# A ring of three-group blocks under the framework's own dependencies in place of hand-made semaphores

## The chip, the cores and the metric

The kernel runs on one core of a Trainium2 chip. The metric is the device time of one execution, in microseconds (us); lower is better. A run that lies over 1.5% above the fastest run of its kernel in the same job counts as slow, and the comparisons use the other, fast, runs.

## The reference, cut to what matters

```python
B, S, D = 8, 4096, 2112          # x is float32
x_r = x.reshape(B, S // 4, 4, D)
pooled = x_r.mean(axis=2)
return x - np.repeat(pooled, 4, axis=1)
```

Four neighbouring rows are averaged and the average is taken off each of them. Input and output are 276.8 MB each.

## The kernel before

A *group* is 128 x 4 rows: each of the 128 partitions holds four rows of 2112 numbers side by side (`W` = 8448). There are 64 groups. SBUF holds a ring of six of them. Three adjacent groups form a *block*, which is loaded and stored in two *pieces* of one and a half groups (6.49 MB each); so the ring holds four pieces. The last four groups go one by one.

```python
blocks = [SUPER] * ((n - TAIL) // SUPER)      # SUPER = 3, TAIL = 4: twenty blocks of three
blocks += [1] * (n - sum(blocks))             # and four singles
...
ring = io_pool.tile([P, RING * W], f32, name="ring")       # RING = 6
s_sb = sum_pool.tile([P, D], f32, name="s_sb")             # sums of even groups, in SBUF
s_ps = psum_pool.tile([P, D], f32, name="s_ps")            # sums of odd groups, in PSUM
```

Loads are issued by SP, stores by ACT, and VectorE (DVE) does all the arithmetic: per group three adds and one *sub*, which multiplies the sum by -1/4 and adds it to the four rows in place. Every wait is written by hand, inside a section that the framework does not touch:

```python
for i, (a, b, src, _, _) in enumerate(moves):          # one load per piece
    ...
    load = nc.sync.dma_start(out=ring[:, a:b], in_=src)
    load._wait_ge(*landed(store_sems, m))              # m: the store that empties this piece
    load.then_inc(load_sems[i % SEMS], 16)
...
for j, (c, need) in enumerate(groups):
    s = s_ps if j % 2 else s_sb
    add = nc.vector.tensor_add(out=s[:], in0=rows[:, 0, :], in1=rows[:, 1, :])
    if need > seen:
        add._wait_ge(*landed(load_sems, need))
    ...                                                # two more adds
    sub = nc.vector.scalar_tensor_tensor(out=rows, in0=..., scalar=-1.0 / STRIDE, in1=rows, ...)
    ...
    store._wait_ge(done_sem, done)                     # a piece leaves when its last sub is done
```

In this section instructions run in the order in which they are written.

## Time and profile before

| | before |
|---|---|
| median of the three runs first made | 1318.18 us (1297.61 to 1322.84) |
| profiled run, span | 1288.6 us |
| VectorE busy | 1023.0 us, 79% |
| load queue + store queue | 49.8% + 49.6% of the DMA engines' time |
| rate, 336 to 1056 us | 434 GB/s |

The lines behind this table are shown in the prediction.

### The profile page before, as it was taken

The numbers are of one execution on the slowest core, as the hardware profiler recorded it, in microseconds if no ns is written. First come the engines' busy times: TensorE is split into PE (matmuls) and PEld (weight loads), VectorE is DVE, ScalarE is ACT, GpSimd is POOL, SyncE is SP. The second block draws the span as 40 slices with busy tenths as digits, with TensorE's granted clock in tenths as the row PEclk, the third lists the DMA queues.
The fourth block names the chain that finished last, engine by engine and source line by source line (L and its number), as shares of the span: only waits on it lengthen the run. The fifth ranks groups of instructions, "written<-read, shape, count | busy, mean of one in ns | idle before, by whom it ended". The sixth has DMA issues, their size and how long they took to land.

```text
span 1288.6 us, 398 instructions
## 1 busy us (share of the span) xinstructions
DVE 1023.0 (79%) x256; POOL 0.2 (0%) x4
## 2 busy tenths in 40 slices
DVE  4999696786969696969688696969696968779864
POOL 0000000000000000000000000000000000000000
DMA  9999999999999999999999999999999999999997
GB/s 403 428 428 434 439 436 428 428 439 437 431 430 434 441 433 428 433 439 434 431 431 439 436 431 430 437 438 431 430 434 442 431 430 431 437 437 425 429 428 325
DMA packets 12674, 553.67 MB, mean 430 GB/s; under 512 B 1408, under 2 KB 1408, under 8 KB 1408
## 3 DMA queue, kind: packets, MB, share of 16 engines
q1 hardware_dynamic: 6336, 276.83, 49.8%
q10 hardware_dynamic: 6336, 276.83, 49.6%
q14 instruction: 2, 0.02, 0.0%
HBM read 276.82 MB, written 276.82 MB: 430 GB/s over the span
## 4 chain that ended last, share of the span: by engine, by line
DMA 66%; DVE 27%; another core or an unknown queue 6%; issue 0%; SPq 0%
DMA out_dram<-ring 35%; DMA ring<-in_x_dram 30%; DVE ring L115 15%; DVE s_ps L111 4%; DVE s_sb L111 4%; DVE s_ps L103 2%; DVE s_sb L103 2%; SPq L89 0%; SPq L161 0%; SPq L80 0%
## 5 line engine op out<-in xcount | busy, mean ns | idle before, releaser
L115 DVE SCALAR_TENSOR_TENSOR ring<-s_sb,ring 128x8448 f32<-128x8448 f32 x32 | 286.7, 8958 | 1.1
L115 DVE SCALAR_TENSOR_TENSOR ring<-s_ps,ring 128x8448 f32<-128x8448 f32 x32 | 286.6, 8957 | 1.1
L103 DVE TENSOR_TENSOR s_sb<-ring 128x2112 f32<-128x2112 f32 x32 | 75.2, 2351 | 132.0 <-DMA ring<-in_x_dram 132.0
L103 DVE TENSOR_TENSOR s_ps<-ring 128x2112 f32<-128x2112 f32 x32 | 75.6, 2362 | 114.3 <-DMA ring<-in_x_dram 114.3
L111 DVE TENSOR_TENSOR s_ps<-s_ps,ring 128x2112 f32<-128x2112 f32 x64 | 151.4, 2366 | 2.2
L111 DVE TENSOR_TENSOR s_sb<-s_sb,ring 128x2112 f32<-128x2112 f32 x64 | 150.9, 2358 | 2.2
L150 POOL MEMSET const-bfloat16-1.0<- 128x1 bf16 x1 | 0.1, 103 | 0.0
L150 POOL MEMSET const-uint8-127<- 128x1 uint8 x1 | 0.1, 102 | 0.0
L150 POOL MEMSET const-float32-0.0<- 128x1 f32 x1 | 0.1, 100 | 0.2 <-issue 0.2
L150 POOL MEMSET const-float32-1.0<- 128x1 f32 x1 | 0.1, 99 | 0.0
## 6 DMA issues: line engine op xcount, KB each, us to landing
ring<-in_x_dram SPq DMA_DIRECT2D x40, 6336.0 KB, 37.4
out_dram<-ring ACTq DMA_DIRECT2D x40, 6336.0 KB, 37.7
ring<-in_x_dram SPq DMA_DIRECT2D x4, 4224.0 KB, 42.7
out_dram<-ring ACTq DMA_DIRECT2D x4, 4224.0 KB, 29.2
```

What stands on the lines that cost most here:

```text
L103: add = nc.vector.tensor_add(out=s[:], in0=rows[:, 0, :], in1=rows[:, 1, :])
L111: add = nc.vector.tensor_add(out=s[:], in0=s[:], in1=rows[:, f, :])
L115: sub = nc.vector.scalar_tensor_tensor(out=rows, in0=s[:, None, :].to_broadcast([P, STRIDE, D]), scalar=-1.0 / STRIDE, in1=rows, op0=mybir ...
L150: nc = _bacc.Bacc("TRN2", target_bir_lowering=False, num_devices=1)
```

## The change

The intent is to hand all synchronization to the framework, which derives waits from what each instruction reads and writes, and to make 21 blocks of three with one single at the end. The diff, cut to its core:

```diff
-TAIL = 4
-SEMS = 8
+TAIL = 1
...
-    with tc.tile_critical():
-        ...                                  # owners, waits and semaphores by hand
+    done = stored = 0
+    for i, (a, b, src, _, _) in enumerate(moves):
+        nc.sync.dma_start(out=ring[:, a:b], in_=src)
+        while done < len(groups) and groups[done][1] <= i:
+            ...
+            s = s_ps if done % 2 else s_sb
+            nc.vector.tensor_add(out=s[:], in0=rows[:, 0, :], in1=rows[:, 1, :])
             for f in range(2, STRIDE):
-                add = nc.vector.tensor_add(out=s[:], in0=s[:], in1=rows[:, f, :])
-                add._wait_ge(done_sem, done)
-                add.then_inc(done_sem)
+                nc.vector.tensor_add(out=s[:], in0=s[:], in1=rows[:, f, :])
-            sub = nc.vector.scalar_tensor_tensor(
+            nc.vector.scalar_tensor_tensor(
                 ...
             )
+            done += 1
+            while stored < len(moves) and moves[stored][4] < done:
+                a, b, _, dst, _ = moves[stored]
+                nc.scalar.dma_start(out=dst, in_=ring[:, a:b])
+                stored += 1
```

Outside the hand-made section the framework also chooses the order of instructions on an engine.

More of the change, by code (lines that the diff above doesn't have):

```diff
@@ L71 @@
     s_ps = psum_pool.tile([P, D], f32, name="s_ps")
-    load_sems = [tc.alloc_semaphore(f"load{i}") for i in range(SEMS)]
-    store_sems = [tc.alloc_semaphore(f"store{i}") for i in range(SEMS)]
-    done_sem = tc.alloc_semaphore("done")
-    def landed(sems, i):
-        return sems[i % SEMS], 16 * (i // SEMS + 1)
-    with tc.tile_critical():
-        owner = {}
-        free = set()
-        for i, (a, b, src, _, _) in enumerate(moves):
-            taken = sorted(
-                {m for (p, q), m in owner.items() if p < b and a < q} - free
-            )
-            for m in taken[:-1]:
-                nc.sync.wait_ge(*landed(store_sems, m))
-            load = nc.sync.dma_start(out=ring[:, a:b], in_=src)
-            for m in taken[-1:]:
-                load._wait_ge(*landed(store_sems, m))
-            load.then_inc(load_sems[i % SEMS], 16)
-            free.update(taken)
-            owner = {c: m for c, m in owner.items() if m not in free}
-            owner[(a, b)] = i
-        done = 0
-        seen = -1
-        stored = 0
-        for j, (c, need) in enumerate(groups):
-            rows = ring[:, c:c + W].rearrange("p (f d) -> p f d", f=STRIDE)
-            s = s_ps if j % 2 else s_sb
-            add = nc.vector.tensor_add(out=s[:], in0=rows[:, 0, :], in1=rows[:, 1, :])
-            assert need <= seen + 1
-            if need > seen:
-                add._wait_ge(*landed(load_sems, need))
-                seen = need
-            add.then_inc(done_sem)
-            done += 1
-            for f in range(2, STRIDE):
-                add = nc.vector.tensor_add(out=s[:], in0=s[:], in1=rows[:, f, :])
-                add._wait_ge(done_sem, done)
-                add.then_inc(done_sem)
-                done += 1
-            sub = nc.vector.scalar_tensor_tensor(
@@ new lines @@
+    done = stored = 0
+    for i, (a, b, src, _, _) in enumerate(moves):
+        nc.sync.dma_start(out=ring[:, a:b], in_=src)
+        while done < len(groups) and groups[done][1] <= i:
+            c = groups[done][0]
+            rows = ring[:, c:c + W].rearrange("p (f d) -> p f d", f=STRIDE)
+            s = s_ps if done % 2 else s_sb
+            nc.vector.tensor_add(out=s[:], in0=rows[:, 0, :], in1=rows[:, 1, :])
+            for f in range(2, STRIDE):
+                nc.vector.tensor_add(out=s[:], in0=s[:], in1=rows[:, f, :])
+            nc.vector.scalar_tensor_tensor(
@@ L122 @@
             )
-            sub._wait_ge(done_sem, done)
-            sub.then_inc(done_sem)
             done += 1
-            while stored < len(moves) and moves[stored][4] <= j:
+            while stored < len(moves) and moves[stored][4] < done:
                 a, b, _, dst, _ = moves[stored]
-                store = nc.scalar.dma_start(out=dst, in_=ring[:, a:b])
-                store._wait_ge(done_sem, done)
-                store.then_inc(store_sems[stored % SEMS], 16)
+                nc.scalar.dma_start(out=dst, in_=ring[:, a:b])
                 stored += 1
-        assert stored == len(moves)
-        for m in sorted(set(range(len(moves))) - free):
-            nc.sync.wait_ge(*landed(store_sems, m))
+    assert done == len(groups) and stored == len(moves)
 _INS = ['x']
```

## The prediction

> **What bounds the kernel now.** I read the page from the top. Engine busy shares come first, then the slices, then the queues.
>
> ```profile
> DVE 1023.0 (79%) x256; POOL 0.2 (0%) x4
> ...
> DMA  9999999999999999999999999999999999999997
> GB/s 403 428 428 434 439 436 428 428 439 437 431 430 434 441 433 428 433 439 434 431 431 439 436 431 430 437 438 431 430 434 442 431 430 431 437 437 425 429 428 325
> ...
> q1 hardware_dynamic: 6336, 276.83, 49.8%
> q10 hardware_dynamic: 6336, 276.83, 49.6%
> ```
>
> Only VectorE (DVE) computes, and it is busy 79% of 1288.6 us. The load queue and the store queue together fill 49.8 + 49.6 = 99.4% of what the 16 DMA engines have. The bytes can't shrink: every input element is read once and every output element written once, 553.7 MB in all. So the transfers are the bound and VectorE has a fifth of its time to spare. The last slice, at 325 GB/s, is the only visibly poor one.
>
> Next I cut the span into stretches, to put a number on the middle and find what is lost at the end (columns: stretch, its length, VectorE busy, POOL busy, TensorE clock, DMA share, GB/s).
>
> ```profile
> 336.00:1056.00 720.00, 576.23 (x145) 0.00 (x0) 1.00 1.00 434
> ...
> 1256.00:1266.00 10.00, 6.27 (x3) 0.00 (x0) 1.00 1.00 433
> 1266.00:1276.00 10.00, 9.79 (x2) 0.00 (x0) 1.00 0.45 193
> 1276.00:1288.60 12.60, 0.00 (x0) 0.00 (x0) 1.00 0.80 343
> ```
>
> The middle runs at 434 GB/s with a DMA share of 1.00. The loss is at 1266 to 1276: 55% of 10 us, 5.5 us, in which the DMA engines have nothing queued because the last group is still on VectorE. The chain of waits in order of time shows the same:
>
> ```profile
> 1255.49 4.16 another core or an unknown queue
> 1259.67 2.38 DVE s_ps L103
> 1262.07 2.38 DVE s_ps L111
> 1264.47 2.38 DVE s_ps L111
> 1266.87 8.96 DVE ring L115
> ```
>
> The last load lands at 1259.65, its group takes 16.2 us, and only then, at 1275.8, is the last store issued. The other three singles' stores are used up before that.
>
> Lastly the waits, first of VectorE and then of the queue that issues loads:
>
> ```profile
> DVE s_sb L103 <- DMA ring<-in_x_dram: 132.0, 11, 18.8
> DVE s_ps L103 <- DMA ring<-in_x_dram: 114.3, 11, 12.4
> ...
> SPq L89 <- DMA out_dram<-ring: 1190.6, 39, 76.6
> ```
>
> VectorE idles only for loads; loads are held only until a store has emptied their piece of the ring. Yet the trace shows a load issued every 29.9 us and landing 37.4 us after issue, so the next load is queued 7.5 us before its predecessor is done. That 7.5 us is the slack any added wait must exceed before the load queue runs dry.
>
> **What the Trainium skill says.** "DMA: Bandwidth & Descriptors", section "Where 436 GB/s comes from", gives 435 GB/s as the ceiling of the SBUF ports; the middle's 434 agrees. The same section says that for transfers from and to HBM about 358 binds; this trace, at 434 both ways together, does not agree, and the measurement decides. Its section "Issuing engines are not separate DMA queues" says that DMAs of all issuing engines run on the same 16 engines and interleave; the two queues' shares summing to 99.4% agree. "VectorE: DVE Perf Modes", section "The DRAIN you can't avoid", says a semaphore between VectorE operations costs nothing extra; the trace agrees in that 128 second and third adds have 2.2 + 2.2 us of idle ahead of them in all. No page says how the framework tracks parts of one buffer; that is my main uncertainty.
>
> **The change, part by part.**
>
> 1. Hand-made semaphores go, the framework's come. Loads stay on SP, stores on ACT, computation on VectorE, in the same ring. Correctness needs the same waits in either kernel: load before adds, subtraction before store, store before the load that reuses the piece. If the framework sees that ring pieces with different columns do not meet, the waits are the same ones. It may add a wait on VectorE beside each load's wait for a store, but that store already waited for VectorE, so it is satisfied on arrival: at most some tenths of a us of SP time (one issue takes 0.33 us there), within the 7.5 us of slack. I count **0 us**.
>
> 2. VectorE's work per group is unchanged: 2.35 + 2 x 2.36 + 8.96 = 16.0 us, 64 groups, 1023 us. Removed waits between its instructions could give at most the 4.4 + 2.2 us of idle named in its rows, on an engine that is not the bound: **0 us**.
>
> 3. The end is reordered. Until block 20 both programs are alike. Before ends with four singles (4.33 MB each); after ends with a block in two pieces of 6.49 MB and one single. At 434 GB/s a piece is 14.95 us of the whole DMA capacity and a single 9.97 us; with both queues active each takes twice that. From the trace: stores of block 19 issue at 1178.0 and 1194.1. In the steady pattern they land 36.1 and 50 us later, 1214.1 and 1244. Block 20's loads issue at 1154.4 and, 29.9 us later, 1184.3; they land at 1191.7 and 1221.7. The single's load issues at 1214.1 (when its slot is emptied), moves from 1221.7 at half rate for 19.9 us, and lands at 1241.6. VectorE: first group of block 20 from 1194.1 to 1210.2; second waits for 1221.7, ends 1237.8 (first store issues); third ends 1253.8 (second store issues); the single ends 1269.9 (last store issues). Stores, alone on the engines after 1241.6: block 19's second done 1242.9, then 1257.9, 1272.8, 1282.8. Each is issued before the one ahead is done (margins 5.1, 4.1 and 2.9 us), so the engines do not run empty. In the trace before, the lone last store took 11.4 us and the span ended 1.3 us after it landed; so 1282.8 + 1.4 + 1.3 = 1285.5. Counting differently, taking the 5.5 us of idle off 1288.6 gives 1283.1. I take **1284.5** for the profiled span, 4 us less.
>
> Sum: 0 + 0 - 4 us, or -0.3%.
>
> **Rivals.** *A: the framework treats the ring as one buffer.* Then a load waits for all earlier stores and VectorE work, and transfers and computation take turns: 1276 (553.7 MB at 434 GB/s) + 1023 = about 2300 us. For it: the ring is one tile, and nothing in the profile excludes it. Against: the code splits pieces by plain column ranges that are easy to tell apart, and it would make the ring pointless. I give it 5%. *B: extra waits or another VectorE order.* If transfers share too few completion semaphores, a load may wait for an unrelated transfer; if the framework puts the next group's adds ahead of a subtraction, a store leaves up to 7.1 us later. Before uses eight each way, and a ring of four pieces never has more than four pieces in any state, so reuse eight transfers on finds the old one landed. A delay under 7.5 us is hidden. Should it be exceeded by 2 us per piece, 43 pieces would cost up to 86 us (+6%), but only if the other queue had nothing to do. Chance 5%. *C: the end becomes VectorE's.* If the single's load lands late, VectorE starts it late, and the margins of 3 to 5 us turn into idle; that would make about 1290, still the same verdict. *D: the time is unchanged and only the chip's scatter shows.* The three runs before are 1322.8, 1297.6 and 1318.2, and the profiled run 1290.4: 2.5% between lowest and highest, eight times my effect. Nothing in the profile explains it and it should touch both kernels.
>
> **Range and chances.** Scaling the median, 1318.2 x 1284.5/1288.6 = 1314.0; scaling the mean of the three (1312.9) gives 1308.7. I choose 1311. The range follows rival D's scatter, 1290 to 1324. Within 2%: 0.84. Slower 0.09, from rivals A and B and scatter. Faster 0.07, scatter alone.
>
> **What would show each step.** Right: the middle at 434 GB/s and share 1.00; loads landing in 37.4 us; no DMA gap near the end until the last store; SP waiting on stores alone. Rival A would show DMA shares far under 0.9 in all slices and VectorE waiting after every piece; B would show the load queue waiting for VectorE or for loads, and GB/s under 430 in the middle; C an idle stretch after 1255. The prediction is wrong if the framework's order or waits differ from the hand-made ones by more than the 7.5 us of slack.

## More of the kernel before

One more view is needed for what follows: the timeline of VectorE where block 19 begins. Columns: start, duration, engine, line, operation, output<-inputs, shapes, count, and in brackets the idle time before it and what ended it. L103 is a group's first add, L111 the other two, L115 the sub.

```profile
1161.87 2.36 DVE L103 TENSOR_TENSOR s_sb<-ring 128x2112 f32<-128x2112 f32 x1 [11.55 <-DMA ring<-in_x_dram]
1164.26 4.75 DVE L111 TENSOR_TENSOR s_sb<-s_sb,ring 128x2112 f32<-128x2112 f32 x2
1169.05 8.96 DVE L115 SCALAR_TENSOR_TENSOR ring<-s_sb,ring 128x8448 f32<-128x8448 f32 x1
1177.92 2.36 DVE L103 TENSOR_TENSOR s_ps<-ring 128x2112 f32<-128x2112 f32 x1
1180.32 4.77 DVE L111 TENSOR_TENSOR s_ps<-s_ps,ring 128x2112 f32<-128x2112 f32 x2
1185.12 8.96 DVE L115 SCALAR_TENSOR_TENSOR ring<-s_ps,ring 128x8448 f32<-128x8448 f32 x1
```

Add, two adds, sub; add, two adds, sub. When VectorE waits for a load (11.55 us here), everything that it was given before that load is already done and its stores are on their way.

## The result, and the profile after

| | before | after |
|---|---|---|
| median of six runs | 1308.61 us (1295.28 to 1322.84) | 1305.83 us (1304.34 to 1307.94) |
| profiled run, span | 1288.6 us | 1304.7 us |
| rate, 336 to 1056 us | 434 GB/s | 429 GB/s |
| VectorE busy | 1023.0 us | 1005.3 us |

The ratio of fast runs, after to before, is 1.0068 (95% interval 1.0039 to 1.0097). It is the mean time of one kernel's fast runs over that of the other's of the same rounds, so not quite the ratio of the medians. The medians are pulled together by slow runs of before; among fast runs the changed kernel is slower by 0.7%, within 2%, and the profiled runs differ by 16.1 us. These 16 us are what has to be explained. The profiled run of before was a quick one (1290.4 us, under all of its six runs), so the usual loss is less: by the ratios here and in the control (run 9), about 9 to 14 us.

Lines of the page of the changed kernel (VectorE busy, DMA share and GB/s in 40 slices, the two queues):

```profile
DVE 1005.3 (77%) x256; POOL 0.2 (0%) x4
...
DMA  9999999999999999999999999999999999999988
GB/s 413 407 448 423 444 421 426 438 406 421 430 440 403 440 429 438 424 427 437 430 416 429 441 412 432 434 427 423 440 427 443 406 439 430 435 417 440 433 350 356
...
q1 hardware_dynamic: 6192, 276.83, 50.1%
q10 hardware_dynamic: 6192, 276.83, 49.0%
```

The DMA engines are still shown as busy nearly everywhere, but they move less: every three or four slices the rate dips to between 403 and 424, and the last two slices are poor. Before, no slice from the second to the 39th is under 425. "Perfetto Trace Analysis" of the Trainium skill, section "Identifying the Most-Contended Engine", says to judge DMA by HBM utilization, since occupancy misleads; here that holds, with a share of nines in both kernels. The same in stretches:

```profile
336.00:1056.00 720.00, 560.53 (x144) 0.00 (x0) 1.00 1.00 429
...
1224.00:1256.00 32.00, 21.29 (x5) 0.00 (x0) 1.00 0.90 390
1256.00:1266.00 10.00, 10.00 (x4) 0.00 (x0) 1.00 0.74 319
1266.00:1276.00 10.00, 10.00 (x3) 0.00 (x0) 1.00 0.76 329
1276.00:1288.60 12.60, 12.51 (x3) 0.00 (x0) 1.00 0.90 386
1288.60:1305.00 16.40, 0.00 (x0) 0.00 (x0) 1.00 0.84 363
```

In the middle (336 to 1056 us) the share is 1.00 and the rate 429. So the engines do not stand idle there; their packets take longer. In the last 80 us they do stand idle, by a tenth to a quarter, and from 1234.7 to 1288.5 us VectorE is busy without a break.

Now the timeline of VectorE at the end of block 19 and the start of block 20 (L77 is a group's first add, L79 the other two, L80 the sub):

```profile
1187.35 2.37 DVE L79 TENSOR_TENSOR s_ps<-s_ps,ring 128x2112 f32<-128x2112 f32 x1
1204.82 2.36 DVE L77 TENSOR_TENSOR s_sb<-ring 128x2112 f32<-128x2112 f32 x1 [15.10 <-DMA ring<-in_x_dram]
1207.09 8.95 DVE L80 SCALAR_TENSOR_TENSOR ring<-s_ps,ring 128x8448 f32<-128x8448 f32 x1
1215.96 2.35 DVE L79 TENSOR_TENSOR s_sb<-s_sb,ring 128x2112 f32<-128x2112 f32 x1
1218.22 2.36 DVE L77 TENSOR_TENSOR s_ps<-ring 128x2112 f32<-128x2112 f32 x1
1220.49 2.35 DVE L79 TENSOR_TENSOR s_sb<-s_sb,ring 128x2112 f32<-128x2112 f32 x1
1234.71 2.37 DVE L79 TENSOR_TENSOR s_ps<-s_ps,ring 128x2112 f32<-128x2112 f32 x1 [11.86 <-DMA ring<-in_x_dram]
1236.99 8.95 DVE L80 SCALAR_TENSOR_TENSOR ring<-s_sb,ring 128x8448 f32<-128x8448 f32 x1
```

The `s_ps` group has its third add done at 1187.35 + 2.37 = 1189.72. Its sub, ready then, runs at 1207.09, 17.4 us later, because the first add of the *next* group (`s_sb<-ring`) stands ahead of it in VectorE's queue and waits for a load until 1204.82. (The Trainium skill, "PSUM — Partial Sum Buffer", section "Engine vs sequencer instructions", says that VectorE's queue is strictly first in, first out; the trace agrees, the ready sub did not pass.) The same happens to the next sub: ready at 1222.84, it runs at 1236.99, behind an add that waits for the second piece of the block. Over groups 12 to 59, a sub started 0.03 us after its third add before, and 6.66 us on average after the change; 16 of those 48 subs were 14.1 to 17.7 us late, the others about 2 us. The total of VectorE's waits for loads grows by 37 us (246 us before, 283 after) but does not say why the time grows: it is what stands behind the waiting add that counts.

Two numbers that I summed from the trace's packet and landing records carry the rest of the argument:

- *Excess of the load packets.* A full packet (50,688 bytes) takes 1.872 us at the median in both kernels. I added up what load packets took above that and divided by the 16 DMA engines: 2.7 us before, 14.3 us after. Store packets stay at 0.3 to 0.4.
- *Lead.* How long before its predecessor on the same queue has landed a transfer is issued, from 200 to 1150 us. Before: loads 7.5 us, stores 6.0 us at the least. After: 8 of 31 stores were issued after their predecessor had landed, that is, onto an empty store queue (up to 3.9 us after). So were 8 of 32 loads, up to 3.8 us after; but around each of these the load packets' excess is 0.15 us or less, with the store queue at work meanwhile. An empty queue alone is therefore not what costs.

The accounts nearly close: 14.3 - 2.7 = 11.6 us by slow packets, and idle DMA time at the end. Before, that is 5.5 us (1266 to 1276) plus 20% of the last 12.6 us, 8.0 us. After, it is 3.2 + 2.6 + 2.4 + 1.3 us in four of the stretches above and 2.6 us in the last, 12.1 us. Together 11.6 + 4.1 = 15.7 of the 16.1 us.

### The profile page after: what moved, and what is told of

The parts are those of the page before. It is cut to its first block, busy times and chain, and to the rows that moved or that the text cites. A ratio compares the mean times of both kernels' runs of the same rounds, so it can differ in the third digit from the quotient of the medians.

```text
span 1304.7 us, 510 instructions
## 1 busy us (share of the span) xinstructions
DVE 1005.3 (77%) x256; POOL 0.2 (0%) x4
## 4 chain that ended last, share of the span: by engine, by line
DMA 61%; DVE 35%; issue 2%; SPq 0%; DVEq 0%
DMA out_dram<-ring 31%; DMA ring<-in_x_dram 30%; DVE ring L80 22%; DVE s_ps L79 6%; DVE s_sb L79 4%; DVE s_ps L77 2%; DVE s_sb L77 2%; SPq L72 0%; DVEq L79 0%
## 5 line engine op out<-in xcount | busy, mean ns | idle before, releaser
L80 DVE SCALAR_TENSOR_TENSOR ring<-s_ps,ring 128x8448 f32<-128x8448 f32 x32 | 286.5, 8953 | 0.1
L80 DVE SCALAR_TENSOR_TENSOR ring<-s_sb,ring 128x8448 f32<-128x8448 f32 x32 | 286.5, 8952 | 0.0
L79 DVE TENSOR_TENSOR s_ps<-s_ps,ring 128x2112 f32<-128x2112 f32 x64 | 151.2, 2363 | 120.1 <-DMA ring<-in_x_dram 120.1
L77 DVE TENSOR_TENSOR s_sb<-ring 128x2112 f32<-128x2112 f32 x32 | 75.3, 2354 | 162.9 <-DMA ring<-in_x_dram 162.9
L79 DVE TENSOR_TENSOR s_sb<-s_sb,ring 128x2112 f32<-128x2112 f32 x64 | 150.6, 2353 | 0.2
L77 DVE TENSOR_TENSOR s_ps<-ring 128x2112 f32<-128x2112 f32 x32 | 75.6, 2362 | 0.0
```

The costliest lines, as they stand in the source:

```text
L79: nc.vector.tensor_add(out=s[:], in0=s[:], in1=rows[:, f, :])
L80: nc.vector.scalar_tensor_tensor(out=rows, in0=s[:, None, :].to_broadcast([P, STRIDE, D]), scalar=-1.0 / STRIDE, in1=rows, op0=mybir.AluOp ...
```

## The experiments

Theory O: the framework's order of VectorE causes the loss, by holding subs back, so that stores leave late. Rivals at first were W (the framework's waits) and T (the new end). All kernels were compared with before on the same chip; the first four ran on one chip, the next four on another, the next three on a third and the last on a fourth. All but the three marked as probes gave the correct result. The theories' letters are those of the expectations; they are not the letters of the prediction's rivals.

**1. The order of before, with the new end** (before with `TAIL = 1`).

```diff
-TAIL = 4
+TAIL = 1
```

> The kernel before with 21 blocks of three and one single, hand-made semaphores and VectorE order kept. If the order of VectorE is the cause (theory O) or the framework's waits are (theory W): the middle stays at 434 GB/s, the excess of the load packets over 1.872 us stays near 2.7 us per DMA engine, and the span is 1283 to 1287 us as predicted for this tail, ratio to before 0.995 to 0.999. If the longer tail itself is the cause (theory T): 1295 us or more, ratio above 1.004.

Measured: median 1292.99 us, ratio 0.9954 (0.9901 to 1.0007), profiled span 1283.4 us.

```profile
336.00:1056.00 720.00, 577.45 (x145) 0.00 (x0) 1.00 1.00 434
...
1266.00:1276.00 10.00, 3.32 (x1) 0.00 (x0) 1.00 0.97 419
```

The middle is untouched, and the hole at 1266 to 1276 (share 0.45 before) is filled. The excess is 2.2 us, every store has at least 6.2 us of lead. The new end alone is worth about 5 us in the profiled run, as the prediction worked out (1284.5), though the interval of the ratio just takes in 1. Theory T, which put the ratio above 1.004, falls.

**2. The changed kernel, with VectorE pinned to program order.**

```diff
-            nc.vector.tensor_add(...)
+            tc.keep_in_program_order(nc.vector.tensor_add(...))     # all adds and the sub
```

> The changed kernel with one thing undone: VectorE's instructions are pinned to program order, the framework's waits stay. Theory O: the time of hand_tail1, span 1283 to 1290 us, middle at 434 GB/s, no sub held behind a later group's add. Theory W: no change, 1302 to 1308 us, middle at 429 GB/s.

Measured: median 1295.85 us, ratio 0.9979 (0.9923 to 1.0036). The loss is gone although all waits are the framework's: theory W falls as the cause of the loss. The interval leaves room for a cost of a few us. The one profiled run was a slow one (1302.6 us), so its trace is not used for durations. Its leads are those of before: 8.5 us or more for stores, 7.4 or more for loads. (The fastest unprofiled run took 1284.95 us.)

**3. Hand-made semaphores, with the framework's order of VectorE.**

```diff
+        order = [(0, 0)]                     # (group, step): 0 to 2 adds, 3 sub
+        for e in range(0, n, 2):
+            order += [(e - 1, 3)] if e else []
+            order += [(e, 1), (e + 1, 0), (e, 2), (e + 1, 1), (e, 3), (e + 1, 2)]
+            order += [(e + 2, 0)] if e + 2 < n else []
+        order.append((n - 1, 3))
-        for j, (c, need) in enumerate(groups):
+        for j, f in order:
```

> The hand-made semaphores with 21 blocks of three and one single, and VectorE's instructions in the interleaved order that the framework chose (each sub behind one or two adds of the next group). Theory O: the loss comes back, span 1300 to 1307 us, middle near 429 GB/s, load packets' excess 10 us or more per engine, VectorE waiting for loads in front of adds whose earlier group's sub is ready. Theory W: 1283 to 1290 us, as hand_tail1.

Measured: median 1315.91 us, ratio 1.0149 (1.0093 to 1.0205), profiled span 1317.7 us; excess 17.5 us; 7 of 30 stores issued onto an empty queue.

```profile
336.00:1056.00 720.00, 558.01 (x143) 0.00 (x0) 1.00 0.99 425
```

The loss comes back without any of the framework's waits, and larger than there. Runs 1 to 3 together settle it: the order, not the semaphores, decides. (From the 17th operation on, VectorE's order in this trace is that of the changed kernel; the first 16 differ a little.) Why this version loses more was not pursued. The packet records show where: over the whole span the DMA engines are idle for 19.4 us and store packets have 2.8 us of excess, against 12.0 and 0.3 in the changed kernel.

**4. The changed kernel with the old end** (`TAIL = 4`).

> The changed kernel with the four singles of before at the end. Theory O and W both leave the middle at 429 GB/s; they differ from theory T, which puts the whole loss in the last 60 us and expects the time of before, 1288 us. O and W: 1298 to 1308 us, the middle's loss of about 11 us remaining, the tail a little better or worse.

Measured: median 1309.36 us, ratio 1.0104 (1.0054 to 1.0153), middle 429 GB/s, excess 16.1 us; the profiled span, 1315.0 us, is above the expected 1298 to 1308. The loss in the middle stays, whatever the end.

**5. Interleaved, but no sub behind a wait.** The order of run 3, except that an add which is first to need a new piece never stands ahead of the previous group's sub. Subs still stand behind an add whose data is there.

```diff
+            early = [x for x in order[:last] if x[0] == j + 1 and piece(*x) > groups[j][1]]
+            if early or ahead:
+                ...                          # the sub first, then those adds
```

> As hand_order, the interleaved order of VectorE, but a sub never stands behind an add that needs a piece not yet landed; it may still stand behind one or two adds whose data is there (up to 4.7 us later). Theory B (the loss is the sub blocked by a wait for a load): as hand_tail1, span 1283 to 1290 us, middle 434 GB/s, load packets' excess in the middle under 2 us per engine. Theory D (the few us of added adds ahead of each sub are enough): loss remains, 1300 us or more, excess 8 us or more.

Measured: median 1285.58 us (1284.86 to 1287.87), ratio 0.9952 (0.9922 to 0.9982), profiled span 1283.8 us. The timeline of VectorE at the same place as above (L147 first add, L152 others, L156 sub):

```profile
1179.13 2.35 DVE L152 TENSOR_TENSOR s_ps<-s_ps,ring 128x2112 f32<-128x2112 f32 x1
1181.52 8.96 DVE L156 SCALAR_TENSOR_TENSOR ring<-s_ps,ring 128x8448 f32<-128x8448 f32 x1
1191.14 2.36 DVE L147 TENSOR_TENSOR s_sb<-ring 128x2112 f32<-128x2112 f32 x1 [0.66 <-DMA ring<-in_x_dram]
```

The sub follows its third add at once, and the wait comes after it. Subs are up to 2.2 us late and nothing is lost: middle 434 GB/s, excess 2.4 us, smallest store lead 5.9 us. So interleaving as such is harmless (theory D falls), and the sub blocked by a wait for a load is the cause (theory B holds).

**6. Late stores with VectorE untouched.** Run 1 with each store held back on ScalarE by small copies. Theory R: what costs is a store issued onto a store queue that has run dry; theory V: VectorE's denser adds slow the load packets directly.

```diff
-                store = nc.scalar.dma_start(out=dst, in_=ring[:, a:b])
-                store._wait_ge(done_sem, done)
+                nc.scalar.wait_ge(done_sem, done)
+                for _ in range(PAUSES):                      # 4 or 12
+                    hold = nc.scalar.copy(out=pause[:], in_=pause[:])
+                    ...
+                store = nc.scalar.dma_start(out=dst, in_=ring[:, a:b])
+                store._wait_ge(late_sem, pauses)
```

> hand_tail1 with VectorE untouched; each store is held on ScalarE by four copies of 1024 PSUM columns after the sub it waits for, about 4 to 5 us by an estimate from one copy of about 1 us. Theory R (the loss comes when a store is issued onto a store queue that has run dry while loads go on): a store was issued 6.2 us ahead of its predecessor's landing, so this is hidden: middle 434 GB/s, span 1284 to 1292 us (4 us may show at the end). Theory V (VectorE's dense adds themselves slow the load packets): the same.

> The same with twelve copies, about 12 to 14 us, above the 6.2 us of lead. Theory R: the store queue runs dry once per block or once per two blocks, the load packets' excess grows to 8 us or more per engine, middle 430 GB/s or less, span 1300 us or more, although VectorE's order is that of before. Theory V: no excess in the middle, 434 GB/s, 1284 to 1300 us from the end alone.

Measured: twelve copies took 12.31 us. With four, median 1297.26 us, ratio 1.0023 (0.9974 to 1.0071), middle 432 GB/s; the span of 1293.4 us lies just above what was expected. With twelve, median 1367.76 us, ratio 1.0509 (1.0462 to 1.0555). A stretch of the latter around one store issue at 301.35:

```profile
292.00:298.00 6.00, 5.93 (x3) 5.81 (x7) 0.00 (x0) 1.00 1.00 431
298.00:302.00 4.00, 4.00 (x1) 3.22 (x4) 0.00 (x0) 1.00 0.68 215
302.00:306.00 4.00, 4.00 (x2) 0.95 (x1) 0.00 (x0) 1.00 0.94 329
306.00:312.00 6.00, 5.93 (x3) 5.81 (x7) 0.00 (x0) 1.00 0.86 355
```

(ScalarE's busy time stands here between VectorE's and POOL's.) With four copies the leads shrink but stay positive (2.1 us at the least). With twelve, 11 of 30 stores and 12 of 30 loads were issued after their predecessor had landed, so this run does not tell late stores from late loads; the load packets' excess is 31.7 us, and engines also stand idle (shares of 0.68 to 0.94). VectorE's order was that of before, so theory V does not explain it.

**7. A probe without VectorE** (wrong result: output = input). A piece is stored when the load two pieces later has landed.

> Wrong result on purpose (output = input): hand_tail1 without any VectorE work; a piece is stored when the load two pieces later has landed, so the store queue runs dry between stores. Theory R: load packets slower than 1.872 us appear around the restarts of the store queue with VectorE idle, excess 8 us or more per engine. Theory V: excess under 3 us, whatever the queues do.

Measured, in a single run: span 1323.8 us, excess 28.8 us, 15 of 31 stores and 16 of 31 loads issued with no lead. Slow load packets appear with no computation at all; and in run 5 VectorE's adds were interleaved too, with only 2.4 us of excess. Theory V falls.

**8. The smallest repair within the framework.** The changed kernel, with the 42 adds that are first to read a piece queued behind the sub before them.

```diff
+                tc.add_manual_dep(add.ins, last_sub.ins.name, ..., reason="sub first")
```

> The changed kernel with one thing added: an add that is the first to read a newly loaded piece is queued behind the sub of the group before it (42 ordering edges, no waits). The rest of the order is left to the framework. Theory B (a sub blocked by a wait for a load is the whole loss): as order_free, span 1283 to 1287 us, middle 434 GB/s, load packets' excess under 4 us per engine. Theory W (something else in the framework's waits also costs): 1290 us or more.

Measured: ratio 0.9971 (0.9904 to 1.0038), fastest run 1284.50 us, middle 433 GB/s, no sub over 2.2 us late, smallest store lead 4.3 us. But three of its six runs were slow, the median is 1303.04 us and the profiled run took 1295.4 us, above the 1283 to 1287 expected. Its load packets' excess, 5.5 us, is also above the expected 4, and store packets have 3.7 us, although no queue ran dry between 200 and 1150 us. By that one trace theory W (1290 us or more) is not excluded. But run 6 with four copies, which has hand-made waits, shows the like (3.9 and 4.0 us), and so does the slow trace of run 2 (7.1 and 4.9 us). So slow packets also come without a dry queue and without the framework's waits; from where was not found. The order is repaired; whether a few us remain is open.

**9. Control: the changed kernel again.**

> The changed kernel once more, as a control on the same chip: 1303 to 1312 us, middle near 429 GB/s, ratio to before 1.005 to 1.015 by every theory.

Measured: median 1306.57 us, ratio 1.0112 (1.0057 to 1.0167), middle 429 GB/s, excess 13.5 us, again 8 of 31 stores without lead.

**10. Two probes of transfers alone** (wrong results). The first keeps a fixed number of loads queued and restarts the store queue beside them.

> Wrong result on purpose: loads and stores alone, no VectorE. Stage 1: twelve loads, three always queued, a store from a fourth piece issued onto an empty store queue at every third. Stages 2, 3 and 4: six loads each, three, two and one queued, no store. Theory R (starting a store on an empty queue slows the loads beside it, however deep the load queue is): stage 1 shows slow load packets after each of its four stores, some 1 us of excess per engine each, stage 2 none. Theory L (a load issued when the load queue is nearly dry is what is slow): stage 1 and 2 none, stage 4 at each load.

Measured: with three loads queued, the first store cost 1.2 us of excess and the other three restarts nothing. (The first store of before and of the changed kernel, near 51 and 55 us, costs about 1 us too; why was not tested.) With two queued and no store, nothing beyond the start of the stage. With one queued, 0.70 to 0.87 us at each load, and 17.4 to 17.9 us from issue to landing instead of one load per 15.0 us. So theory R, as put, is too simple: restarts beside a deep load queue were hidden.

The second issues a load c, a store, or both onto the tail of a load b:

> Wrong result on purpose: 14 trials of transfers alone. In each, loads a and b go out together; after a has landed and 1, 5, 9, 11 or 13 ScalarE pauses of 1.03 us (an estimate from the held stores' run), a load c, or c and a store at once, or a store alone is issued onto the tail of b, whose remaining time is about 15 us less the pauses. Theory L (a transfer issued with little left in the queues stretches its first packets): excess near 0 at 1, 5 and 9 pauses, 0.7 us or more per engine at 13, for c alone. Theory E (it takes both, a load and a store issued together onto almost empty queues): near 0 for c alone at every lead, 1 us or more for the pair at 11 and 13. Theory R (a store onto an empty queue, whatever the lead): 1 us or more in every trial with a store.

Load packets' excess per engine, from the issue until all had landed. What b had left unshared is the lead measured in the trials with c alone. Each figure is one trial.

| pauses (b has left) | 1 (12.6 us) | 5 (9.8 us) | 9 (5.6 us) | 11 (3.6 us) | 13 (1.5 us) |
|---|---|---|---|---|---|
| c alone | 0.00 | 0.01 | 0.01 | 0.16 | 0.81 |
| c and a store | 1.18 | 1.19 | 1.27 | 3.17 | 3.61 |
| a store alone | 0.96 | 1.12 | 1.01 | 0.16 | not run |

In the two short pair trials the store packets lost 1.8 and 1.6 us as well. So a load alone costs nothing when it is issued 5.6 us before the queue needs it, little at 3.6 us and 0.8 us at 1.5 us. Restarting the store queue costs about 1 us of load time while a load is under way with at most one more behind it. Both together, onto nearly empty queues, cost several us. Theory L and theory E each hold in part.

The changed kernel is in a situation like it. Once per two blocks, about every 121 us, a load is issued 3.6 to 3.7 us before its predecessor lands and a store follows 2 to 4 us later onto the empty store queue. Eight such places between 216 and 1150 us hold 10.5 of the 11.3 us of load excess there: 0.8 to 2.1 us each, less than the pair cost in the probe, where both were issued at once. One of them, in the changed kernel:

```profile
644.00:652.00 8.00, 8.00 (x3) 0.00 (x0) 1.00 1.00 431
652.00:656.00 4.00, 4.00 (x2) 0.00 (x0) 1.00 0.99 406
656.00:660.00 4.00, 4.00 (x2) 0.00 (x0) 1.00 0.99 291
660.00:668.00 8.00, 8.00 (x4) 0.00 (x0) 1.00 1.02 444
```

A load is issued at 651.70 and a store at 655.59; for 4 us the rate falls to 291 GB/s at a share of 0.99.

What stays open: what happens inside a DMA engine during a stretched packet; where the slow packets of runs without a dry queue come from; and what makes single runs of most kernels up to 3% slower (the six runs of run 5 lie within 0.3%).

| kernel | sub late by (mean) | smallest store lead | load excess | middle | ratio to before |
|---|---|---|---|---|---|
| before | 0.03 us | 6.0 us | 2.7 us | 434 GB/s | 1 |
| after | 6.7 us | none (8 of 31) | 14.3 us | 429 GB/s | 1.0068 |
| hand order, new end | 0.03 us | 6.2 us | 2.2 us | 434 GB/s | 0.9954 |
| hand waits, framework's order | 6.7 us | none (7 of 30) | 17.5 us | 425 GB/s | 1.0149 |
| same, sub never behind a wait | 1.1 us | 5.9 us | 2.4 us | 434 GB/s | 0.9952 |
| stores held 12.3 us | 0.03 us | none (11 of 30) | 31.7 us | 410 GB/s | 1.0509 |

The fifth row is the one version whose fast runs are clear of both: 0.5% under before, with an interval below 1, and 1.1% or more under the changed kernel by the ratios to before.

## Why the prediction was right or wrong

- *The bound is the transfers.* Right. The best versions (runs 1 and 5) run at 434 GB/s in the middle and end at 1283.4 to 1283.8 us, where the packets alone, at 1.872 us each, need 1278.0.
- *The number.* 1305.83 lies in the range and "within 2%" was right. But 1311 rested on a median that held slow runs; fast runs of before are near 1297 us. The step from before to after was forecast as -0.3% and measured as +0.7% in the first comparison, +1.1% in the control. That 1305.83 came so near to 1311 is luck: the base behind it, about 1315, was some 18 us above before's fast runs, and the slowdown that was not foreseen filled half of the gap.
- *Step 1, the framework's waits, 0 us.* Right: 0.9979 with the order pinned.
- *Step 2, VectorE's work, 0 us.* This is the step that failed. It counted durations and forgot order. VectorE's busy time fell by 17.7 us, more than the 4.4 + 2.2 us allowed for, because independent operations start before the previous one has ended (1207.09 against 1204.82 + 2.36 in the timeline above). And yet its order cost about 11.6 us in packets, and the end besides.
- *Step 3, the end, -4 us.* Right by itself: 1283.4 measured in run 1 for the predicted 1284.5, 5.2 us under before, and the last three stores issued at 1237.2, 1253.3 and 1269.3 us for the predicted 1237.8, 1253.8 and 1269.9. In the changed kernel it was undone: the second piece of block 20 landed at 1234.7, not at 1221.7; from then VectorE worked without a break to 1288.5, and its subs came late. That is close to rival C, brought about by the order; but it was block 20's second piece that landed late for VectorE, not the single.
- *Rival B* named the mechanism and mis-sized it. It put a sub at most 7.1 us late and hid that under the load queue's 7.5 us. Measured were 14 to 18 us for a third of the subs, because the add ahead was waiting for a load; and the slack that counted was the store queue's 6 us. With a chance of 5% it was rated too low.
- *Rival A* did not occur: pieces of one ring are told apart.
- *The signs.* The prediction said that rival B would show as GB/s under 430 in the middle. It did: 429. Rival B's other sign did not show: the load queue waited for stores alone, as before. Rival C's did, an idle stretch after 1255 us. And the prediction's own test of being wrong, an order that differs by more than the 7.5 us of slack, was met by subs 14 to 18 us late.

## What to carry to other kernels

When a framework orders an engine's queue, read that order in the timeline: an instruction that waits for data must not stand ahead of finished work that other queues are waiting for. For a transfer-bound kernel, watch how long before its predecessor lands each transfer is issued; a share of 1.00 can hide a queue that ran dry. Here 42 ordering edges, about one per piece, kept every sub ahead of the add that waits, under the framework's own waits; whether all of the time came back was not shown.

## What the Trainium skill lacked or had wrong

- "DMA: Bandwidth & Descriptors", section "Where 436 GB/s comes from", says without a condition that the HBM side, about 358 GB/s, binds for transfers between HBM and SBUF. The page's note under its measured table gives that figure for both cores of an HBM domain streaming; the sentence lacks this, and the prediction took it for a contradiction. Here a program on one core moved 434 GB/s, loads and stores together, through 720 us.
- The same page's section "Queues, rings and completion order" describes how engines alternate between queues, but not what a queue that is empty or nearly so costs in slower packets: 0.8 us for a load issued alone, 1.5 us ahead of need, about 1 us for restarting the store queue, 3.2 to 3.6 us (and 1.6 to 1.8 us of store packets) for both at once.
- No page has what a framework's own order on an engine can cost: here an add that waited for a load, placed ahead of a ready sub, made 16 of 48 subs 14 to 18 us late.
